# A down product of 22 feature tiles, 16 of them regrouped into seven products of quarters

## The chip, the core and the metric

The kernel runs on one NeuronCore of a Trainium2 chip. A time is device microseconds (us) of one execution. The core's engines run at the same time and wait for each other by semaphores: TensorE (PE in the profile: matmuls into PSUM, weight loads as PEld), VectorE (DVE), ScalarE (ACT), GpSimd (POOL) and SyncE (SP). Each takes its instructions strictly in the order in which they stand in its queue. SP and POOL also issue transfers (DMA) between DRAM and the on-chip buffers.

## The reference

Two layers on 512 tokens of width 1024. Each layer has a mixer (convolution and windowed attention, or gated linear attention and latent attention), a layer norm, a SwiGLU feed-forward network with 2816 hidden features, and a second layer norm:

```python
def swiglu(x, w_gate, w_up, w_down):
    return (jax.nn.silu(x @ w_gate) * (x @ w_up)) @ w_down

x = layer_norm(ALPHA * x + y, ln_mix_g[layer], ln_mix_b[layer])
x = layer_norm(ALPHA * x + swiglu(x, ffn_w_gate[layer], ffn_w_up[layer], ffn_w_down[layer]),
               ln_ffn_g[layer], ln_ffn_b[layer])
```

The change is in the last factor, `@ w_down`, of both layers: 512 tokens x 2816 features times 2816 x 1024.

## The kernel before

All arithmetic is float32. A product of two float32 tiles is made of three matmuls in a reduced 32-bit format: each operand is split into an upper part `hi` (a cast on ACT) and a lower part `lo` = operand - `hi` (a subtraction on DVE), and hi*hi, hi*lo and lo*hi are added up in PSUM. `split` (lines 96 to 104) does that: its ACT row stands at L98, its DVE row at L104. A weight tile is 128 x 1024: `weight()` fetches it from DRAM on SP into one of the 5 buffers of the pool `raw` (RAW), takes one of the 5 pairs of the pool `w` (WP) and splits it. A feature tile of the hidden activations is 128 features x 512 tokens; its parts go to the pool `hx` (HX, 12 buffers).

The feed-forward network of a layer has two stages.

- Gate and up (`ffn`, `sevens`). The first two feature tiles (DIRECT) are plain products. The other 20 are taken in ten pairs, each by Winograd's form of Strassen's method: seven products of quarters in place of eight, with sums of weight quarters and of input quarters ahead of them. `make(i)` prepares product i: a sum of weights on DVE (L531, L525), then the split. `take(i)` issues its matmuls (L553) and moves the results between PSUM banks on ACT and DVE. The loop calls `make(i)` and then `take(i - 4)` (AHEAD), so the preparation runs up to four products ahead; `make(i)` also needs the `w` pair that product i - 5 has given back. This whole stage is under `tc.manual_schedule`: the instructions of every engine stand in the order in which the code is written.
- Down (`down`). The 22 feature tiles come one by one in groups `[1] * 17 + [5]`. For each tile `prep` splits the tile and its 128 x 1024 weight tile; then for 4 blocks of 128 tokens and 2 halves of 512 columns three matmuls (L336, in `one`) add into one of 8 PSUM banks, 24 matmuls for a tile. The last group has five tiles, so that the layer norm of one block of tokens runs beside the matmuls of the next.

PE's matmuls always stand in the order of the code. The weights lie in DRAM in the order in which the kernel fetches them; `_chunks` puts them there before the launch.

## Time and profile before

| | |
|---|---|
| median of 3 runs | 1075.84 us (1075.57 to 1076.06) |
| the profiled execution | 1075.87 us; span of its instructions 1074.1 us |
| granted TensorE clock | 0.999 |
| PE busy | 1064.4 us (99%), 6957 matmuls |
| DVE, ACT, POOL busy | 726.7 us (68%), 497.9 us (46%), 61.3 us (6%) |
| transfers | 110.44 MB, 103 GB/s on average |
| matmuls of the down products and of the mixers' output products (L336) | 1425, 326.0 us busy |

How to read it: busy time is the union of an engine's instructions; matmuls overlap in the pipeline, so the mean length of one (390 ns) is longer than the step from one to the next. In the rows of a timeline stand start and length in us, engine, line, operation, output <- input, shape, count, and in brackets the time for which the engine stood idle before it and what ended that. The chain of waits follows the work that ended last back to the start, each step to what released it.

### The profile page before, as it was taken

The numbers are of one execution on the slowest core, as the hardware profiler recorded it, in microseconds if no ns is written. First come the engines' busy times: TensorE is split into PE (matmuls) and PEld (weight loads), VectorE is DVE, ScalarE is ACT, GpSimd is POOL, SyncE is SP. The second block draws the span as 40 slices with busy tenths as digits, with TensorE's granted clock in tenths as the row PEclk, the third lists the DMA queues.
The fourth block names the chain that finished last, engine by engine and source line by source line (L and its number), as shares of the span: only waits on it lengthen the run. The fifth ranks groups of instructions, "written<-read, shape, count | busy, mean of one in ns | idle before, by whom it ended". The sixth has DMA issues, their size and how long they took to land.

```text
span 1074.1 us, 17049 instructions
## 1 busy us (share of the span) xinstructions
PE 1064.4 (99%) x6957; PEld 962.6 (90%) x6957; DVE 726.7 (68%) x1128; ACT 497.9 (46%) x832; POOL 61.3 (6%) x98
## 2 busy tenths in 40 slices
PE   9999999999999999999999999999999999999997
PEld 7888889999999998888988888889999999988886
DVE  5666539897787783334857886479977777753337
ACT  5544335654544562223467453355645545542221
POOL 0000000000000000000513420000000000000001
PEclk9999999999999999999999999999999999999999
DMA  9522221333323343331332031223423323442302
GB/s 337 202 79 79 79 79 59 99 99 124 113 80 120 116 161 115 98 99 59 99 137 78 2 118 30 77 71 80 147 89 108 117 90 107 156 134 96 98 1 78
DMA packets 32078, 110.44 MB, mean 103 GB/s; under 512 B 3568, under 2 KB 4224, under 8 KB 32000
## 3 DMA queue, kind: packets, MB, share of 16 engines
q1 hardware_dynamic: 31712, 108.31, 30.5%
q0 software_dynamic: 288, 1.05, 0.6%
q8 instruction: 54, 0.88, 0.3%
q14 instruction: 24, 0.20, 0.1%
HBM read 107.25 MB, written 2.10 MB: 102 GB/s over the span
## 4 chain that ended last, share of the span: by engine, by line
PE 97%; DVE 1%; DMA 0%; ACT 0%; issue 0%; SPq 0%; POOL 0%; DVEq 0%; ACTq 0%; POOLq 0%
PE ps L553 38%; PE ps L336 29%; PE ps L180 16%; PE ps L214 6%; PE ps L1005 1%; PE ps L276 1%; PE ps L930 1%; PE ps L853 1%; PE ps L702 1%; PE ps L649 1%; PE ps L689 1%; DMA hx<-in_xT_dram 0%; PE ps L903 0%; PE ps L919 0%; PE ps L901 0%; PE ps L1080 0%
## 5 line engine op out<-in xcount | busy, mean ns | idle before, releaser
L336 PE MATMUL ps<-w,hx 128*128 128x512 f32 x1425 | 326.0, 390 | 0.0
L336 PEld LDWEIGHTS ps<-w,hx 128*128 128x128 f32 x1425 | 266.7, 188 | 55.0
L104 DVE TENSOR_TENSOR w<-raw,w 128x1024 fp32r<-128x1024 f32 (+2 forms) x182 | 219.9, 1213 | 63.9 <-ACT w L98 58.1
L553 PE MATMUL ps<-xh,w 128*128 128x256 f32 x1280 | 237.5, 283 | 0.0
L98 ACT CAST w<-raw 128x1024 fp32r<-128x1024 f32 (+3 forms) x185 | 189.6, 1032 | 60.4 <-PE ps L553 21.1
L553 PEld LDWEIGHTS ps<-xh,w 128*128 128x128 f32 x1280 | 202.7, 192 | 0.0
L553 PE MATMUL ps<-xl,w 128*128 128x256 f32 x640 | 181.2, 283 | 0.0
L553 PE MATMUL ps<-hx,w 128*128 128x256 f32 x1440 | 179.6, 283 | 0.0
L553 PEld LDWEIGHTS ps<-hx,w 128*128 128x128 f32 x1440 | 176.0, 192 | 0.1
L180 PE MATMUL ps<-xh,w 128*128 128x512 f32 (+1 forms) x608 | 161.0, 348 | 0.1
L553 PEld LDWEIGHTS ps<-xl,w 128*128 128x128 f32 x640 | 122.8, 192 | 0.3
L180 PEld LDWEIGHTS ps<-xh,w 128*128 128x128 f32 x608 | 106.4, 189 | 15.2 <-ACT xh L98 0.5
L180 PE MATMUL ps<-xl,w 128*128 128x512 f32 (+1 forms) x304 | 104.9, 345 | 0.2 <-DVE xl L104 0.2
L104 DVE TENSOR_TENSOR hx<-m,hx 128x512 fp32r<-128x512 f32 x32 | 21.4, 688 | 81.4 <-ACT hx L98 81.4
L180 PEld LDWEIGHTS ps<-xl,w 128*128 128x128 f32 x304 | 57.6, 190 | 7.0 <-DVE xl L104 0.5
L253 POOL TENSOR_TENSOR rs<-ve,neghalf 128x1 f32<-128x1 f32 x15 | 9.5, 635 | 866.7 <-DVE ve L251 828.8
L214 PE MATMUL ps<-w,xh 128*128 128x512 f32 (+1 forms) x192 | 58.6, 386 | 0.3 <-ACT lng L909 0.3
L98 ACT CAST hx<-m 128x512 fp32r<-128x512 f32 x32 | 19.2, 623 | 83.3 <-PE ps L336 83.1
L104 DVE TENSOR_TENSOR hx<-wk,hx 128x512 fp32r<-128x512 f32 x28 | 19.3, 691 | 51.8 <-ACT hx L98 51.8
L104 DVE TENSOR_TENSOR w<-lng,w 128x1024 fp32r<-128x1024 f32 x30 | 36.8, 1225 | 21.1 <-ACT w L98 21.1
L104 DVE TENSOR_TENSOR w<-lnb,w 128x1024 fp32r<-128x1024 f32 x30 | 36.8, 1225 | 17.4 <-ACT w L98 17.3
L98 ACT CAST hx<-wk 128x512 fp32r<-128x512 f32 x28 | 17.4, 622 | 64.0 <-PE ps L336 61.4
(229 smaller groups left out, 1112.2 us busy)
## 6 DMA issues: line engine op xcount, KB each, us to landing
raw<-in_w_dram SPq DMA_DIRECT2D x182, 512.0 KB, 4.1
hx<-in_xT_dram SPq DMA_DIRECT2D x8, 256.0 KB, 5.5
xn<-in_xn_dram SPq DMA_DIRECT2D x4, 512.0 KB, 9.4
out_dram<-xn SPq DMA_DIRECT2D x7, 256.0 KB, 2.0
lng<-in_ln_mix_g_dram SPq DMA_DIRECT2D x2, 512.0 KB, 7.9
lnb<-in_ln_mix_b_dram SPq DMA_DIRECT2D x2, 512.0 KB, 8.0
raw<-in_w_dram POOLq DMA_DIRECT2D x2, 512.0 KB, 5.6
lng<-in_ln_ffn_g_dram SPq DMA_DIRECT2D x2, 512.0 KB, 6.9
```

The source lines that it names most:

```text
L98: nc.scalar.copy(out=hi, in_=src)
L104: tt(out=lo, in0=src, in1=hi.bitcast(F32), op=ALU.subtract)
L180: mm(dst[:, cols], lhsT=l[:, k, :], rhs=r[:, k, cols], start=(k == 0 and n == 0), stop=(k == KD - 1 and n == 2))
L214: mm(banks[b][:, :n], lhsT=l[:, k, t], rhs=r[:, c], start=(k == 0 and m == 0), stop=(k == KD - 1 and m == 2))
L276: nc.tensor.transpose(tp[:, k * P:(k + 1) * P], xn[:, b, h * 512 + k * P:h * 512 + (k + 1) * P], ident)
L336: mm(acc[b][h], lhsT=l[:, bs], rhs=r[:, h * 512:h * 512 + 512], start=(k == 0 and n == 0), stop=(k == ends[b, h] and n == 2))
L553: mm(bank[:, f * 256:f * 256 + 256], lhsT=l[:, f, k, :], rhs=r[k // 2][:, k % 2, :], start=(start and f == 0 and k == 0 and m == 0), stop= ...
L649: mm(banks[s][bank][:, o:o + n], lhsT=l[rows[s], b * P:(b + 1) * P], rhs=r[rows[s], (b + 1) * P - n:(b + 1) * P], start=(i == 0), stop=(i ...
L689: nc.tensor.transpose(bank[:, o:o + P], src, ident)
L702: mm(po[rows[s], b * P:(b + 1) * P], lhsT=vn[:, j * P + 64 * s:j * P + 64 * s + 64], rhs=loc[s][(b, half)], start=(half == 0 or b == 0), s ...
L853: mm(dst, lhsT=x[:, c], rhs=y, start=(k == 0 and n == 0), stop=(k == nk - 1 and n == 2))
L930: mm(po[:, e * P:(e + 1) * P], lhsT=vv[j - 1 if j else i][:, h * P:(h + 1) * P], rhs=pt[e][:, j * P:(j + 1) * P], start=(j == 0), stop=(j ...
```

## The change

Of the 22 feature tiles, tiles 2 to 17 (16 tiles, 4 * QUADS) are no longer taken one by one. They make a product of 512 tokens x 2048 features x 1024 columns, which is cut into quarters: tokens in two halves of 256, features in two halves of 8 tiles, columns in two halves of 512. With A for the hidden activations and B for the weights, the seven products of Winograd's form are each summed over four groups (q = 0 to 3) of two feature tiles, 28 small products in all, in the order of the list `seq` of pairs (pos, q). `seven_down` holds it. A small product is 12 matmuls of 128 x 512 (2 blocks of tokens, 2 feature tiles, 3 parts). The sums over q stay in PSUM, and the sums between the seven products are made by continuing in a bank: after the last product of pos 6, ACT copies the two banks `d` to two banks `e` (L619) and the products of pos 3 go on in `d`; after the last of pos 7 it copies `e` to `f`, and pos 4 goes on in `f`. The sums of activation quarters are made on DVE (L581 to L588) in every `make` of pos 5, 6, 3 and 7, ahead of the split of the sum. The sums of weight quarters are running sums: after the split of one stage, a transfer on POOL's queue with `accum_op=ALU.add` adds the next quarter from DRAM to the same buffer (`add`, 16 transfers of 512 KB in a layer). The buffers of the running weight sums and of the activation sums are those of `xh` and `xl`, which is why these are now two tiles each (`xk`, `renew`). The six other feature tiles follow in `down` in groups `[1, 5]`, added to the same banks. The hidden tiles of a pair are kept as one tile for each half of the tokens, so that `half` is one instruction, not two. The first two loads of `seven_down` (`raw` of ("21", 0) and ("21", 1)) are issued when `seven_down` is called, which is before the loop over the gate and up products; the layer norm's `load_ln` moves into the loop.

```diff
+QUADS = 4
...
-    def down(hs, groups, gb, last=False, after=None, keep=None):
+    def down(hs, groups, gb, last=False, after=None, keep=None, acc=None):
...
-        nk = len(hs)
-        acc = {}
+        nk = sum(groups)
+        begun = acc is not None
+        acc = acc if begun else {}
...
-                if gi == 0:
+                if gi == 0 and not begun:
                     acc[b] = [ps(), ps()]
...
-            for i in range(AHEAD + 3, n + AHEAD):
+            acc, more, takes = seven_down(hs)
+            for i in range(AHEAD + 3, n + len(more) + AHEAD):
                 if i < n:
                     make(i)
-                take(i - AHEAD)
-        gb = load_ln("ffn", layer)
-        return down(hs, [1] * (KF - 5) + [5], gb, last)
+                elif i < n + len(more):
+                    more[i - n]()
+                    if i == n + 3:
+                        gb = load_ln("ffn", layer)
+                i -= AHEAD
+                if i < n:
+                    take(i)
+                else:
+                    takes[i - n]()
+        rest = [h for h in hs[:DIRECT]] + [h for h in hs[DIRECT + 2 * QUADS:]]
+        return down(rest, [1, 5], gb, last, acc=acc)
+
+    def seven_down(hs):
...
+        seq = [(2, 0), (2, 1), (1, 0), (1, 1), (2, 2), (5, 0), (1, 2), (5, 1), (1, 3), (2, 3), (5, 2), (6, 0),
+               (5, 3), (6, 1), (6, 2), (6, 3), (3, 0), (3, 1), (3, 2), (3, 3), (7, 0), (7, 1), (7, 2), (7, 3),
+               (4, 0), (4, 1), (4, 2), (4, 3)]
...
+        def add(t, which, q):
+            nc.gpsimd.dma_start(out=t, in_=piece(which, q), accum_op=ALU.add)
...
+        def make(i):
+
+            for args in loads.get(i, ()):
+                load(*args)
+            pos, q = seq[i]
+            (a11, a21), (a12, a22) = hs[DIRECT + q], hs[DIRECT + QUADS + q]
+            w = raw["21", q] if pos == 2 else raw["22", q] if pos in (3, 7) else t_[q]
+            hi, lo = pair()
+            split(w, hi, lo)
+            if pos in (1, 5, 6, 3):
+                add(w, {1: "12", 5: "22", 6: "21", 3: "12"}[pos], q)
+            hh, hl = slot2(F32R), slot2(F32R)
+            x = {1: a11, 2: a12, 4: a22, 7: None}.get(pos, s_.get(q))
+            if pos == 5:
+                tt(out=x, in0=a22, in1=a21, op=ALU.subtract)
+            elif pos == 6:
+                tt(out=x, in0=x, in1=a11, op=ALU.add)
+            elif pos == 3:
+                tt(out=x, in0=x, in1=a12, op=ALU.subtract)
+            elif pos == 7:
+                x = temp()
+                tt(out=x, in0=a11, in1=a21, op=ALU.subtract)
...
+                split(x, hh, hl)
+            ops[i] = hi, lo, hh, hl
+
+        def take(i):
...
+                if pos == 5:
+                    g.setdefault("p5", []).append(temp("p"))
+                    nc.scalar.copy(out=g["p5"][b], in_=bank)
+                elif pos in (6, 7):
+                    to = "e" if pos == 6 else "f"
+                    g.setdefault(to, []).append(ps())
+                    nc.scalar.copy(out=g[to][b], in_=bank)
+            if q == QUADS - 1:
+                for b in range(2):
+                    if pos == 1:
+                        g["p1"] = temp()
+                        nc.scalar.copy(out=g["p1"], in_=g["d"][b])
+                        g.setdefault("sum", []).append((b, g["p1"]))
+                    elif pos in (3, 7):
+                        bank = g[name][b]
+                        stt(out=bank, in0=bank, scalar=-1.0, in1=g["p5"][b], op0=ALU.mult, op1=ALU.subtract)
+            if pos == 2 and q == QUADS - 1:
+                for b, t in g["sum"]:
+                    tt(out=g["a"][b], in0=g["a"][b], in1=t, op=ALU.add)
...
-                for f in range(2):
-                    c = slice(f * 256, f * 256 + 256)
-                    stt(out=g["h"][f][:, n * 256:n * 256 + 256], in0=gate[:, c], scalar=-1.0, in1=up[:, c],
-                        op0=ALU.mult, op1=ALU.mult)
+                stt(out=g["h"][n], in0=gate, scalar=-1.0, in1=up, op0=ALU.mult, op1=ALU.mult)
```

Three engines, each at one place of the first layer's down stage. In these rows `w` is a weight pair, `hx` a part of an activation tile, `wk` a hidden tile, `ssum` an activation sum, `tsum` a running weight sum, `ps` a PSUM bank. The lines of the changed kernel differ from those of the profile before: its split stands at L99 and L105, its small products at L609.

ACT before, in the middle of the tiles taken one by one: the upper parts of an activation tile and of a weight tile in turn.

```order
L98 CAST hx_4478<-wk_2831 128x512
L98 CAST w_4451<-raw_4449 128x1024
L98 CAST hx_4511<-wk_2832 128x512
L98 CAST w_4484<-raw_4482 128x1024
L98 CAST hx_4544<-wk_3059 128x512
L98 CAST w_4517<-raw_4515 128x1024
```

ACT now, from the `make` of (3, 0) to that of (7, 0):

```order
L99 CAST w_4499<-raw_4401 128x1024
L99 CAST hx_4503<-ssum_4080 128x512
L615 COPY p_4514<-ps_4345 128x512
L615 COPY p_4522<-ps_4346 128x512
L99 CAST w_4524<-raw_4428 128x1024
L99 CAST hx_4528<-ssum_4080 128x512
L99 CAST w_4545<-raw_4453 128x1024
L99 CAST hx_4549<-ssum_4228 128x512
L99 CAST w_4566<-raw_4476 128x1024
L99 CAST hx_4570<-ssum_4228 128x512
L619 COPY ps_4581<-ps_4283 128x512
L619 COPY ps_4589<-ps_4284 128x512
```

The copies of `d` to `e` (L619) belong to the `take` of (6, 3), the 16th product, and stand in ACT's queue behind both casts of the `make` of (3, 3), the 20th; the cast of each activation sum stands ahead of the cast of the next weight.

DVE before, at the same tiles as ACT above:

```order
L104 TENSOR_TENSOR hx_4479<-wk_2831,hx_4478 128x512
L104 TENSOR_TENSOR w_4451<-raw_4449,w_4451 128x1024
L104 TENSOR_TENSOR hx_4512<-wk_2832,hx_4511 128x512
L104 TENSOR_TENSOR w_4484<-raw_4482,w_4484 128x1024
L104 TENSOR_TENSOR hx_4545<-wk_3059,hx_4544 128x512
```

DVE now, from the `make` of (6, 2) to that of (3, 0):

```order
L105 TENSOR_TENSOR w_4455<-tsum_4227,w_4455 128x1024
L583 TENSOR_TENSOR ssum_4228<-ssum_4228,wk_2605 128x512
L591 SCALAR_TENSOR_TENSOR hx_4460<-ssum_4228,hx_4459 128x512
L105 TENSOR_TENSOR w_4478<-tsum_4227,w_4478 128x1024
L583 TENSOR_TENSOR ssum_4228<-ssum_4228,wk_2831 128x512
L591 SCALAR_TENSOR_TENSOR hx_4483<-ssum_4228,hx_4482 128x512
L105 TENSOR_TENSOR w_4499<-raw_4401,w_4499 128x1024
L585 TENSOR_TENSOR ssum_4080<-ssum_4080,wk_3057 128x512
L105 TENSOR_TENSOR hx_4504<-ssum_4080,hx_4503 128x512
```

Each `make` now has three instructions on DVE, and the activation sum (L583, L585) stands behind the lower part of the weight and ahead of the lower part of the sum itself.

PE now, the end of (6, 3) and the start of (3, 0); before, the eight banks took 24 matmuls of one tile in turn, with no copy between:

```order
L609 MATMUL ps_4284<-w_4478,hx_4482 128x512 x2
L609 MATMUL ps_4284<-w_4478,hx_4483 128x512
L609 MATMUL ps_4284<-w_4478,hx_4482 128x512 x2
L609 MATMUL ps_4284<-w_4478,hx_4483 128x512
L609 MATMUL ps_4283<-w_4499,hx_4503 128x512 x2
L609 MATMUL ps_4283<-w_4499,hx_4504 128x512
```

(3, 0) goes on in the banks `ps_4283` and `ps_4284` that the copies of L619 read.

## The prediction

> **What bounds the kernel now.** I read the page first, then the chain of waits in order of time, then the timelines of ACT and DVE.

> ```profile
> span 1074.1 us, 17049 instructions
> PE 1064.4 (99%) x6957; PEld 962.6 (90%) x6957; DVE 726.7 (68%) x1128; ACT 497.9 (46%) x832; POOL 61.3 (6%) x98
> L336 PE MATMUL ps<-w,hx 128*128 128x512 f32 x1425 | 326.0, 390 | 0.0
> ```

> ```profile
> 219.39 181.43 PE ps L553 x1512
> 400.82 110.19 PE ps L336 x486
> 946.54 106.12 PE ps L336 x468
> ```

> PE is the bound: it is busy 99% of the span, and the matmuls of the down product wait for nothing (0.0 us idle). In the chain, 486 of them take 110.19 us, 0.2267 us each; in the second layer it is 0.2268. A gate and up product takes 24 x 181.43 / 1512 = 2.88 us. So time is saved by fewer matmuls, as long as ACT and DVE keep their operands coming. How they do that in the down stage now:

> ```profile
> 401.41 1.04 ACT L98 CAST w<-raw 128x1024 fp32r<-128x1024 f32 x1
> 406.10 0.62 ACT L98 CAST hx<-wk 128x512 fp32r<-128x512 f32 x1 [3.65 <-PE ps L336]
> 406.63 1.05 ACT L98 CAST w<-raw 128x1024 fp32r<-128x1024 f32 x1
> 411.54 0.62 ACT L98 CAST hx<-wk 128x512 fp32r<-128x512 f32 x1 [3.87 <-PE ps L336]
> ```

> ```profile
> 406.76 0.69 DVE L104 TENSOR_TENSOR hx<-wk,hx 128x512 fp32r<-128x512 f32 x1 [3.02 <-ACT hx L98]
> 407.70 1.23 DVE L104 TENSOR_TENSOR w<-raw,w 128x1024 fp32r<-128x1024 f32 x1 [0.26 <-ACT w L98]
> 412.20 0.69 DVE L104 TENSOR_TENSOR hx<-wk,hx 128x512 fp32r<-128x512 f32 x1 [3.27 <-ACT hx L98]
> ```

> One tile every 5.44 us (406.10 to 411.54), and both engines stand idle for over 3 us of it, waiting for PE. This slack is what the change spends.

> **What is saved on PE.** 16 tiles x 24 = 384 matmuls become 28 x 12 = 336: 48 fewer in a layer, 96 in all, of the same shape (128 x 512). 96 x 0.2268 = 21.8 us. A small product takes 12 x 0.2268 = 2.72 us.

> **What the preparation costs.** It must now be done every 2.72 us. The trace has the new order of work at one place, where the gate and up stage makes its input sums (DVE L414, two tiles at a time) between two weight splits:

> ```profile
> 201.34 1.28 DVE L414 TENSOR_TENSOR p<-m 128x512 f32<-128x512 f32 x2
> 204.27 1.22 DVE L104 TENSOR_TENSOR w<-raw,w 128x1024 fp32r<-128x1024 f32 x1 [0.26 <-ACT w L98]
> 205.41 1.28 DVE L414 TENSOR_TENSOR p<-tmp,m 128x512 f32<-128x512 f32 x2
> ```

> ```profile
> 202.06 1.23 ACT L98 CAST hx<-p 128x512 fp32r<-128x512 f32 x2
> 203.19 1.05 ACT L98 CAST w<-raw 128x1024 fp32r<-128x1024 f32 x1
> ```

> Sum to its cast 0.72 us; two casts 1.13 us; the weight cast to its lower part 1.08 us; that to the next sum 1.14 us; 4.07 us from sum to sum. The new `make` has one tile, whose cast takes 0.53 us (406.10 to 406.63), so its ring is 0.72 + 0.53 + 1.08 + 1.14 = 3.47 us. It is a ring since both engines take their work in order: the sum stands behind the previous weight on DVE, and the next weight's cast behind the sum's cast on ACT. 16 of the 28 makes have a sum (pos 5, 6, 3, 7), and those from the 11th to the 24th stand together, except for copies between. Each is 3.47 - 2.72 = 0.75 us slower than PE.

> That alone would eat up the lead of four products and no more. But the 17th product, (3, 0), waits for the copy of `d` to `e`, and that copy stands on ACT behind the whole make of the 20th. At this place the lead is worth nothing. Rows for the extra work:

> ```profile
> 383.58 0.57 ACT L580 COPY ps<-ps 128x512 f32<-128x512 f32 x1 [1.29 <-PE ps L553]
> 384.06 1.05 ACT L98 CAST w<-raw 128x1024 fp32r<-128x1024 f32 x1
> 397.98 1.05 ACT L98 CAST w<-raw 128x1024 fp32r<-128x1024 f32 x1 [0.22 <-PE ps L553]
> ```

> ```profile
> 398.24 0.68 DVE L601 TENSOR_TENSOR p<-p,ps 128x512 f32<-128x512 f32 x1
> 398.84 0.69 DVE L104 TENSOR_TENSOR hx<-wk,hx 128x512 fp32r<-128x512 f32 x1
> ```

> A copy holds ACT for 0.48 us, an add with PSUM holds DVE for 0.60 us. The cast at 397.98 starts 0.06 us after the product that frees its pair (the 69th of 70, which ended 2.88 us before 400.82): the preparation is at its full lead when the down stage starts. I count from the end of the gate and up products (t = 0). Up to the 11th make the lead holds: only two of those ten have a sum, and each loses 0.8 us that the next plain ones give back. So the 11th starts when the 6th product has freed its pair, at 6 x 2.72 + 0.08 = 16.4. Its sum's cast is at 16.4 + 1.08 + 1.14 + 0.72 = 19.34. Nine rings on, 9 x 3.47 = 31.23, stands the 20th's; on the way two copies `p1` (0.96) and two copies `p5` (0.96) stretch the ring on ACT, and two adds to `a` on DVE: the lower part of the sum ends 0.66 + 0.60 after its cast (406.10, 406.76), the adds 1.20 later, at 2.46, where the next weight could have gone at 0.53 + 1.08 = 1.61, so 0.85. Sum 53.34. With that cast (0.53) and the copy (0.57) PE may start (3, 0) at 54.4. It ended the 16th product at 16 x 2.72 = 43.5. **PE stands still for 10.9 us in each layer**, 21.8 us in all, which is what the matmuls save. After it PE is ahead of nothing: by then the 20th make is done, four products are ready, the rest follow at 3.47 and later (pos 4, without a sum) at some 1.75 us, before PE asks for them; the copy to `f` has 1.36 us of the other block's matmuls beside it.

> **What the standstill does to the clock.** Start and end of the program show it.

> ```profile
> 1.45 5.87 PE L147 MATMUL ps<-hx 128*128 128x512 f32 x14 [1.45 <-DVE hx L145]
> 1062.68 3.75 PE L306 MATMUL ps<-w,hx 128*128 128x256 f32 x30
> ```

> ```profile
> 1066.00:1070.00 4.00, 0.43 (x4) 1.00 0.05 20
> 1070.00:1074.00 4.00, 0.00 (x0) 0.70 0.38 133
> ```

> The last matmul ends at 1066.4, and in the last stretch the granted clock (the column behind PE's) is 0.70 on average: it fell to half some 5 us after the last matmul (0.4 of 4 us at 1, the rest at 0.5). The first 14 matmuls after a standstill take 0.42 us each, not 0.227. An idle time of 10.9 us is long enough, so the first dozen matmuls after it run at half speed: 12 x (0.427 - 0.227) = 2.4 us, taking 5.87 us as the time to recover and 0.427 for a fully slow one; twice 4.8 us. Bounds: 0 if the clock stays up, 2.8 us (14 x 0.2) each. [...]

> **Transfers.** Running sums go over POOL's queue.

> ```profile
> raw<-in_w_dram SPq DMA_DIRECT2D x182, 512.0 KB, 4.1
> raw<-in_w_dram POOLq DMA_DIRECT2D x2, 512.0 KB, 5.6
> ```

> ```profile
> 189.00:190.00 1.00, 1.00 (x11) 1.00 (x10) 1.00 (x2) 1.00 (x2) 0.00 (x0) 1.00 0.95 168
> 190.00:191.00 1.00, 1.00 (x11) 1.00 (x10) 0.74 (x2) 0.98 (x2) 0.00 (x0) 1.00 1.07 213
> ```

> An adding transfer lands after 5.6 us and keeps the DMA engines busy for some 3 us (share about 1, from 188 to 191). Needed sooner than 5.6 us? A transfer starts when the lower part of its weight is done, 1.08 + 1.14 us after that make's start. The tightest are (1, 0) to (5, 0), started at -3.5 (its make at -2 x 2.88 + 0.08) and needed at 2.8 (the sixth make, one product freed), and (1, 2) to (5, 2), 8.5 to 16.4. Alone they fit, by 0.7 and 2.3 us. But up to there seven plain loads and four adding ones want the same DMA engines. I take 0 for this term; the other end is 4 us in a layer.

> The two `raw` buffers taken early leave three for the gate and up products. A quarter is then loaded only when one of the previous group is split, two or three products (5.8 to 8.6 us) before its use, against 4.1 us to landing: 0, and if the cover goes, up to 1 us for each of 8 groups. `half` in one instruction, `load_ln` earlier, the 12 more weight splits: beside PE, or inside the ring counted above. POOL's later work (one power for each block of the layer norm) comes some 20 us after its last transfer. The last groups `[1, 5]`: their five preparations wait for the same pairs as before, 0.

> **Sum**, against the profiled 1075.87 us (0.03 over the median): 1075.9 - 21.8 + 21.8 + 4.8 = 1080.7, say 1081 us.

> **Rivals.**
> - *PE never waits* (the other side). If the ring does not close, DVE's own load decides: 1.14 + 2 x 0.60 = 2.34 us for a make with a sum, under 2.72. Then only the copy on ACT shows, about 1.4 us in a layer: 1075.9 - 21.8 + 2.8 = 1057. For it: DVE's idle 3 us of 5.44. Against it: the 0.26 us wait for ACT within the ring above. It decides if the ring is under some 3.1 us: 9 x (3.47 - 3.1) takes 3.3 us off the wait, and wait and clock then cost under 10 us in a layer.
> - *The wait comes, the clock does not fall*: 1076, no change. For it: only a start and an end show the clock, no pause. Against: 10.9 us is twice the 5 us of the end.
> - *The adding transfers come late*: 4 us more in a layer, 1089. For it: the shares of about 1; against: most of them have 8 us and more.
> - *Three buffers starve the gate and up stage*: 16 us more, 1097. Against it: SP waits 381 us in all for free buffers there now, and PE never waits for a load.

> ```profile
> SPq L506 <- DVE w L104: 381.1, 60, 21.8
> ```

> **Chances.** The forecast 54%, PE never waits (or waits less than half of it) 12%, clock stays up 14%, late transfers 15%, starved stage 5%. The range: a ring of 3.35 to 3.6 us changes the wait by 1.3 us a layer, the clock term by up to 0.8, transfers add up to 4 us a layer; with the second rival that is 1074 to 1091; the first and the last rival lie outside. Faster or slower by under 0.2% (2.2 us) is about what a measurement of this kernel cannot tell from no change: the second rival lies within it, with a part of the low end of the forecast. Faster 0.13, same 0.18, slower 0.69.

> **What would show it.** Right: in each down stage one idle time of PE of 9 to 13 us ahead of the first product of pos 3, ended by ACT's copy at L619; a dip of the granted clock behind it; sums on DVE 3.4 to 3.6 us apart before it; no other wait of PE over 1 us. Wrong: DVE's sums 2.7 us apart; PE idle while ACT waits for a transfer to `tsum`; the gate and up products longer than 2.88 us; the clock at 1.00 behind the wait.

## The result, and the profile after

The changed kernel takes 1089.1 us (median of 4 runs, 1088.67 to 1089.22) against 1075.7 us before on the same chip: ratio 1.0123, 95% interval 1.0106 to 1.0141, slower by 13.4 us. The forecast was 1081, 5.2 us slower, with a range to 1091. The profiled execution took 1089.05 us. Its page, and the group of the down product's small products:

```profile
span 1087.2 us, 17047 instructions
PE 1049.5 (97%) x6861; PEld 947.1 (87%) x6861; DVE 791.2 (73%) x1180; ACT 544.1 (50%) x896; POOL 89.2 (8%) x130
q1 hardware_dynamic: 30560, 104.12, 29.3%
q0 software_dynamic: 4896, 17.83, 9.3%
L609 PE MATMUL ps<-w,hx 128*128 128x512 f32 x672 | 159.9, 400 | 27.9 <-ACT ps L619 23.5
```

There are 96 matmuls fewer, as forecast, but PE now stands idle for 27.9 us ahead of these products, 23.5 of them until ACT's copy at L619. PE's timeline shows where (start, length, count, and in brackets the idle time before and what ended it), both layers:

```profile
400.44 30.11 PE L609 MATMUL ps<-w,hx 128*128 128x512 f32 x132
432.70 11.58 PE L609 MATMUL ps<-w,hx 128*128 128x512 f32 x48 [2.15 <-ACT tmp L624]
444.45 3.32 PE L609 MATMUL ps<-w,hx 128*128 128x512 f32 x12 [0.17 <-ACT hx L590]
459.73 34.45 PE L609 MATMUL ps<-w,hx 128*128 128x512 f32 x144 [11.97 <-ACT ps L619]
...
952.64 30.11 PE L609 MATMUL ps<-w,hx 128*128 128x512 f32 x132
984.78 15.49 PE L609 MATMUL ps<-w,hx 128*128 128x512 f32 x60 [2.03 <-ACT tmp L624]
1011.81 34.86 PE L609 MATMUL ps<-w,hx 128*128 128x512 f32 x144 [11.54 <-ACT ps L619]
```

The first product of pos 3 starts 59.3 us after the gate and up products (t = 459.73 - 400.44), not 54.4. The 144 matmuls behind the wait take 34.45 and 34.86 us instead of 144 x 0.2268 = 32.66: 1.8 and 2.2 us lost to the clock (granted 0.50 until 462.99 and until 1015.95 us, 3.3 and 4.1 us after the product starts). A second idle time of 2 us, ahead of the product that waits for the copy `p1` (L624), was not in the forecast. The chain of waits, followed back through layer 0, says what lies behind both:

```profile
401.08 10.80 DMA tsum<-in_w_dram
411.98 1.06 ACT w L99
...
418.05 10.44 DMA tsum<-in_w_dram
428.59 1.07 ACT w L99
...
454.48 0.61 DVE ssum L585
455.64 1.05 ACT w L99
456.72 1.23 DVE w L105
459.73 34.45 PE ps L609 x144
```

Its last part is the ring of the forecast. Its first part is two adding transfers that took 10.8 and 10.4 us until their weight's cast could start; the forecast had taken 0 for them. ACT's timeline shows all five casts of layer 0 that a transfer held up, the fourth of them that of the 11th make (the second waits for a plain load on SP's queue, the others for adding transfers):

```profile
404.06 1.05 ACT L99 CAST w<-tsum 128x1024 fp32r<-128x1024 f32 x1 [1.31 <-DMA tsum<-in_w_dram]
408.30 1.05 ACT L99 CAST w<-tsum 128x1024 fp32r<-128x1024 f32 x1 [0.67 <-DMA tsum<-in_w_dram]
411.98 1.05 ACT L99 CAST w<-tsum 128x1024 fp32r<-128x1024 f32 x1 [2.11 <-DMA tsum<-in_w_dram]
421.08 1.05 ACT L99 CAST w<-tsum 128x1024 fp32r<-128x1024 f32 x1 [2.60 <-DMA tsum<-in_w_dram]
428.59 1.06 ACT L99 CAST w<-tsum 128x1024 fp32r<-128x1024 f32 x1 [0.47 <-DMA tsum<-in_w_dram]
```

The 11th make starts at t = 421.08 - 400.44 = 20.6 instead of 16.4.

### The profile page after: what moved, and what is told of

It is laid out like the page before. It is cut to its first block, busy times and chain, and to the rows that moved or that the text cites. A ratio compares the mean times of both kernels' runs of the same rounds, so it can differ in the third digit from the quotient of the medians.

```text
span 1087.2 us, 17047 instructions
## 1 busy us (share of the span) xinstructions
PE 1049.5 (97%) x6861; PEld 947.1 (87%) x6861; DVE 791.2 (73%) x1180; ACT 544.1 (50%) x896; POOL 89.2 (8%) x130
## 3 DMA queue, kind: packets, MB, share of 16 engines
q0 software_dynamic: 4896, 17.83, 9.3%
## 4 chain that ended last, share of the span: by engine, by line
PE 86%; DVE 5%; DMA 5%; ACT 3%; issue 1%; SPq 0%; POOL 0%; DVEq 0%; ACTq 0%; POOLq 0%
PE ps L712 35%; PE ps L189 15%; PE ps L345 13%; PE ps L609 7%; PE ps L223 6%; DMA tsum<-in_w_dram 4%; DVE w L105 2%; ACT w L99 2%; PE ps L1161 1%; PE ps L285 1%; PE ps L1086 1%; PE ps L1009 1%; PE ps L858 1%; PE ps L805 1%; PE ps L845 1%
## 5 line engine op out<-in xcount | busy, mean ns | idle before, releaser
L105 DVE TENSOR_TENSOR w<-raw,w 128x1024 fp32r<-128x1024 f32 (+2 forms) x174 | 210.0, 1211 | 60.3 <-ACT w L99 55.7
L99 ACT CAST w<-raw 128x1024 fp32r<-128x1024 f32 (+3 forms) x177 | 181.4, 1032 | 65.7 <-PE ps L712 18.1
L609 PE MATMUL ps<-w,hx 128*128 128x512 f32 x672 | 159.9, 400 | 27.9 <-ACT ps L619 23.5
L609 PEld LDWEIGHTS ps<-w,hx 128*128 128x128 f32 x672 | 129.1, 193 | 58.1 <-ACT ps L619 24.4
L345 PE MATMUL ps<-w,hx 128*128 128x512 f32 x657 | 151.9, 391 | 0.0
L345 PEld LDWEIGHTS ps<-w,hx 128*128 128x128 f32 x657 | 122.7, 188 | 25.1
L559 POOL DMA_DIRECT2D tsum<-in_w_dram x24 | 20.9, 871 | 493.4 <-DVE w L105 282.1
L105 DVE TENSOR_TENSOR w<-tsum,w 128x1024 fp32r<-128x1024 f32 x32 | 39.2, 1224 | 18.1 <-ACT w L99 18.1
L105 DVE TENSOR_TENSOR w<-lng,w 128x1024 fp32r<-128x1024 f32 x30 | 36.7, 1223 | 17.1 <-ACT w L99 16.9
L105 DVE TENSOR_TENSOR w<-lnb,w 128x1024 fp32r<-128x1024 f32 x30 | 36.7, 1223 | 15.0 <-ACT w L99 14.9
L105 DVE TENSOR_TENSOR hx<-m,hx 128x512 fp32r<-128x512 f32 x32 | 21.4, 689 | 31.8 <-ACT hx L99 31.8
## 6 DMA issues: line engine op xcount, KB each, us to landing
raw<-in_w_dram SPq DMA_DIRECT2D x166, 512.0 KB, 4.3
tsum<-in_w_dram POOLq DMA_DIRECT2D x24, 512.0 KB, 8.4
raw<-in_w_dram POOLq DMA_DIRECT2D x10, 512.0 KB, 5.7
tsum<-in_w_dram SPq DMA_DIRECT2D x8, 512.0 KB, 6.3
xn<-in_xn_dram SPq DMA_DIRECT2D x4, 512.0 KB, 9.4
lng<-in_ln_mix_g_dram SPq DMA_DIRECT2D x2, 512.0 KB, 7.7
```

What stands on the lines that cost most here:

```text
L99: nc.scalar.copy(out=hi, in_=src)
L105: tt(out=lo, in0=src, in1=hi.bitcast(F32), op=ALU.subtract)
L345: mm(acc[b][h], lhsT=l(b), rhs=r[:, h * 512:h * 512 + 512], start=(not begun and k == 0 and n == 0), stop=(k == ends[b, h] and n == 2), sk ...
L559: nc.gpsimd.dma_start(out=t, in_=piece(which, q), accum_op=ALU.add)
L609: mm(bank, lhsT=l[:, t], rhs=r[:, c], start=(fresh and k == 0 and m == 0), stop=(k == 1 and m == 2), skip_group_check=True)
```

## The experiments

Ten kernels, in three sets; each set ran on one chip beside the kernel before, and each ratio is to that. (Between the sets the median of the kernel before varies from 1075.5 to 1076.1 us, so a difference between two sets can be off by some 0.5 us.) e1 to e6 start from the changed kernel, e7 to e10 from e4.

| run | what it changes | us (median) | ratio to before (95%) |
|---|---|---|---|
| e1 | no adding transfers | 1081.5 | 1.0047 (1.0032 to 1.0061) |
| e2 | the loads of the quarters 22 later | 1083.6 | 1.0066 (1.0049 to 1.0082) |
| e3 | the copies d to e ahead of the 19th make | 1089.3 | 1.0122 (1.0106 to 1.0137) |
| e4 | the ring opened | 1060.2 | 0.9846 (0.9831 to 0.9861) |
| e5 | plain transfers in place of adding ones | 1081.4 | 1.0051 (1.0036 to 1.0066) |
| e6 | matmuls in PE's standstill | 1085.4 | 1.0091 (1.0075 to 1.0106) |
| e7 | e4, and (2, 3) later | 1065.4 | 0.9898 (0.9882 to 0.9915) |
| e8 | e7 and e2 | 1056.4 | 0.9823 (0.9808 to 0.9838) |
| e9 | e4 and e2 | 1063.2 | 0.9884 (0.9866 to 0.9902) |
| e10 | e9, and the copies d to e ahead of the 20th make | 1054.8 | 0.9813 (0.98 to 0.9827) |

**e1, without the adding transfers.**

```diff
-            if pos in (1, 5, 6, 3):
+            if False:
                 add(w, {1: "12", 5: "22", 6: "21", 3: "12"}[pos], q)
```

> The adding transfers are left out, so the running weight sums are not formed and the output differs; every other instruction stands where it stood in the changed kernel. Theory (the adding transfers make the 11th make of a down stage late): no cast of a summed weight waits for a transfer, the 11th make starts at t = 16.4 instead of 20.6 us after the gate and up products, the first product of pos 3 at t = 54 instead of 59.3; 2 x 4.9 us less, with the smaller clock loss 1077 to 1081 us. What is left against the kernel before (PE standing still for 11 us and the clock behind it) stays. Rival (the lateness comes from the load on ACT and DVE, not from transfers): 1086 to 1090 us.

1081.5 us, 7.6 less than the changed kernel (8.0, if each is compared with the kernel before in its own set). PE's waits and its timeline in layer 0:

```profile
PE ps L609 <- ACT ps L619: 21.9, 2, 11.0
```

```profile
400.78 43.71 PE L609 MATMUL ps<-w,hx 128*128 128x512 f32 x192
455.46 34.95 PE L609 MATMUL ps<-w,hx 128*128 128x512 f32 x144 [10.97 <-ACT ps L619]
```

The first 16 products run without a pause, pos 3 starts at t = 54.7, and PE stands still for 21.9 us in all: the 54.4 and the 21.8 of the forecast. The clock behind the two waits (granted 0.986 over this run, 0.998 to 0.999 before) costs 2.3 us here (34.95 - 32.66) and 3.0 in layer 1 (35.70 us for 144 matmuls). So the ring and the copy behind it were sized right, and what the sum lacked came with the transfers.

**e2 and e5, why the transfers are late.** e2 leaves all transfers in and moves four plain loads; e5 leaves all of them where they are and takes only the adding away.

```diff
-            nc.sync.dma_start(out=raw[which, q], in_=piece(which, q))
+            (nc.gpsimd if which == "22" else nc.sync).dma_start(out=raw[which, q], in_=piece(which, q))
```

> Only the four plain loads of the quarters 22 move, from SP's queue, where all four start within 4 us after the gate and up products, to POOL's, where each stands behind the adding transfer of the make before it (the 12th to 15th). All transfers are made. Theory (adding transfers land late because these plain loads share the DMA engines with them): the adding transfers of the first 20 us land in 6 to 8 us instead of 8.4 and more, the 11th make starts 2 to 4 us earlier, 1081 to 1085 us. Rival (an adding transfer is itself that slow, or is delayed by the three plain loads that stay and by POOL): the wait of the 11th make stays over 2 us, 1087 to 1090 us.

```diff
-            nc.gpsimd.dma_start(out=t, in_=piece(which, q), accum_op=ALU.add)
+            nc.gpsimd.dma_start(out=t, in_=piece(which, q))
```

> The 24 adding transfers become plain ones of the same 512 KB, on the same queue, at the same places, with the same waits; the weight sums are not formed, so the output differs. Theory (it is the time that adding takes on the DMA engines, 328 ns for a 4 KB piece against 159 ns for a plain one in the trace of the changed kernel, that fills them in the first 20 us): they land in 5 to 7 us instead of 8.4, casts no longer wait for them by more than 1 us, 1080 to 1084 us. Rival (the number of transfers and their bytes fill the queue, adding or not): the 11th make stays 3 us or more late, 1087 to 1090 us.

1083.6 and 1081.4 us: both recover most of it, e5 as much as leaving the transfers out, with landings even earlier than the 5 to 7 us expected. The transfers' rows (KB each, median us from issue to landing) of the changed kernel, e2 and e5, in this order:

```profile
tsum<-in_w_dram POOLq DMA_DIRECT2D x24, 512.0 KB, 8.4
```

```profile
tsum<-in_w_dram POOLq DMA_DIRECT2D x24, 512.0 KB, 6.8
```

```profile
q0 software_dynamic: 4896, 17.83, 5.1%
tsum<-in_w_dram POOLq DMA_DIRECT2D x24, 512.0 KB, 4.1
```

The rows count the 24 transfers of a run that add to `tsum`; eight more add to `raw` (pos 3), and e1 and e5 concern all 32, not 24 as was expected of e5. So neither theory's rival holds, and the two theories are one: it is a matter of the engines' time. The page gives the mean length of a packet: 9.3% x 16 engines x 1087.2 us / 4896 packets = 330 ns for a queue of nearly only adding transfers; in e5, with the same packets and bytes, 5.1% x 16 x 1078.2 / 4896 = 180 ns. One packet in nine has only 4 bytes; of the 4 KB pieces alone the median in the changed kernel's trace is 328 ns adding (POOL's queue) and 159 ns plain (SP's). A transfer of 512 KB is 128 pieces, so some 2.6 us of all 16 engines against 1.4. (POOL's own time to issue one, 0.87 us against 0.54 in e5, is too small a difference to make up the 4.3 us between the landings.) The windows of layer 0 from 400 to 430 us (last columns: granted clock, busy share of the DMA engines, GB/s), of the changed kernel:

```profile
400.00:410.00 10.00, 10.00 (x49) 8.34 (x48) 6.99 (x9) 5.29 (x7) 1.75 (x2) 1.00 0.98 232
410.00:420.00 10.00, 10.00 (x46) 8.29 (x45) 7.20 (x9) 4.61 (x6) 2.62 (x3) 1.00 1.05 288
420.00:430.00 10.00, 10.00 (x46) 8.29 (x45) 5.45 (x8) 4.32 (x5) 1.74 (x2) 1.00 1.06 266
```

The DMA engines are full (shares of 0.98 to 1.06). An estimate from these lengths: from 398.3, when the first of them is issued, to 421.1, when the 11th make starts, six adding transfers (6 x 2.64 = 15.8 us) and seven plain loads (7 x 128 x 0.167 / 16 = 9.4 us, from q1's row) ask for 25.2 us in 22.8. By the trace's packets, pieces of 4.6 adding and 6.0 plain transfers were begun in that stretch and took 21.9 us of the 16 engines; the rest had to wait. Taking four plain loads out (5.3 us) brings the demand under the time there is, and so does plain in place of adding (6 x 1.2 = 7.2 us), with more to spare: in e2 one cast of layer 0 and three of layer 1 still wait 0.3 to 1.5 us for a transfer to `tsum`, in e5 none.

**e3, the copies earlier.**

```diff
+                if i == n + 18:
+                    for j in range(n + 14, n + 16):
+                        takes[j - n]()
...
-                else:
+                elif not n + 14 <= i < n + 16:
                     takes[i - n]()
```

> Only the place of the copies d to e (with the products (6, 2) and (6, 3) on PE, whose order stays) moves, from behind the 20th make to ahead of the 19th. Theory (the first product of pos 3 waits for a copy that stands on ACT behind makes that have nothing to do with it, and these run at 3.47 us each): the copy starts 6.9 us earlier (452.2 instead of 459.1), the product with it; later makes then come 0.6 to 0.8 us late each for the next products, so 10 to 14 us less in all, 1075 to 1080 us. Rival (ACT and DVE are simply too slow for 28 makes, wherever the copy stands): PE waits as long as before, only at other products; 1086 to 1090 us.

1089.3 us: no gain, though pos 3 does start 7 us earlier (the copy is L622 here). PE's group and its layer 0:

```profile
L612 PE MATMUL ps<-w,hx 128*128 128x512 f32 x672 | 165.4, 408 | 22.2 <-ACT ps L622 17.7 <-ACT tmp L627 4.3 <-ACT hx L593 0.2
```

```profile
452.43 24.59 PE L612 MATMUL ps<-w,hx 128*128 128x512 f32 x96 [5.05 <-ACT ps L622]
481.03 12.77 PE L612 MATMUL ps<-w,hx 128*128 128x512 f32 x48 [4.01 <-ACT ps L622]
```

The time came back twice. PE now reaches the end of pos 7 before the copy of `e` to `f`, which stands on ACT behind the last makes, those of pos 7 and pos 4: 4.0 us of idle time that the late start had hidden. And there are two waits of 4 to 5 us instead of one of 12, each followed by matmuls at half clock (granted 0.50 from 450.70 to 457.53 and from 481.42 to 484.83 us): 24.59 - 96 x 0.2268 = 2.8 us and 12.77 - 48 x 0.2268 = 1.9 us, against 1.8 once. In all, 5.7 us less idle (22.2 for 27.9) and 5.5 us more busy (165.4 for 159.9). My expectation had followed the ring to the 24th make and forgotten the second copy behind it. By time alone this run fits the rival, "too slow wherever the copy stands"; e4 refutes that.

**e4, the ring opened.** The same instructions; only the sum of the next make stands ahead of this make's lower part on DVE.

```diff
-            split(w, hi, lo)
+            nc.scalar.copy(out=hi, in_=w)
+            if i + 1 < len(seq) and seq[i + 1][0] in (5, 6, 3, 7):
+                xs[i + 1] = sum_of(*seq[i + 1])
+            tt(out=lo, in0=w, in1=hi.bitcast(F32), op=ALU.subtract)
```

> The activation sum of the next make is put on DVE ahead of the lower part of this make's weight, so the cast of a sum on ACT no longer waits for it; same instructions, same number. Theory (the ring sum, cast, next weight's cast, its lower part limits, at 3.47 us, and not what the engines have to do): sums come 2.3 to 2.8 us apart, PE waits at most 1 to 5 us in a layer (the copy d to e and what the late transfers leave), the clock stays up, 1055 to 1064 us, faster than both kernels. Rival (DVE with three or four passes in a make, or ACT, is itself the bound): sums still 3.2 us or more apart, 1080 us or more.

1060.2 us, faster than both kernels. DVE's sums, first of the changed kernel, then of e4:

```profile
450.94 0.69 DVE L585 TENSOR_TENSOR ssum<-ssum,wk 128x512 f32<-128x512 f32 x1
454.40 0.69 DVE L585 TENSOR_TENSOR ssum<-ssum,m 128x512 f32<-128x512 f32 x1
```

```profile
440.54 0.68 DVE L575 TENSOR_TENSOR ssum<-ssum,wk 128x512 f32<-128x512 f32 x1
442.88 0.69 DVE L575 TENSOR_TENSOR ssum<-ssum,m 128x512 f32<-128x512 f32 x1
```

3.46 us apart with the ring, 2.34 without: the forecast's figure for DVE's own load (1.14 + 2 x 0.60). The transfers are no earlier here (8.9 us to landing, casts wait up to 5.7 us for them), but a preparation that takes 2.34 us for a product of 2.72 regains its lead, and only the copy d to e (L628) is left to wait for, as PE's waits show (us in total, times, longest):

```profile
PE ps L618 <- ACT ps L628: 4.2, 2, 2.1
```

**e6, what the clock cost.** 40 matmuls whose results nobody reads fill most of the standstill.

```diff
+                    elif pos == 6 and b == 1:
+                        for j in range(40):
+                            mm(g["b"][j % 2], lhsT=hh[:, :P], rhs=hi[:, :512], start=True, stop=True)
```

> 40 matmuls of the same shape, whose results nothing reads, stand on PE between the 16th product and the first of pos 3 (some 9.1 us of the 12 in which it stands still). Theory (the clock falls because PE rests): no dip of the granted clock behind the wait, the 144 matmuls after it take 32.7 us instead of 34.5 and 34.9, the start of the first product of pos 3 stays where it was: 3 to 5 us less, 1084 to 1086 us. Rival (the clock is not what makes these matmuls long): 1088 to 1090 us.

1085.4 us, 3.7 less. The product of pos 3 starts when it did (t = 59.2), and its 144 matmuls take 32.94 us; in the window in which the 40 run, the granted clock (the column ahead of the DMA share) stays at 1.00:

```profile
448.11 9.63 PE L628 MATMUL ps<-w,hx 128*128 128x512 f32 x40 [0.17 <-ACT p L615]
459.47 32.94 PE L609 MATMUL ps<-w,hx 128*128 128x512 f32 x144 [1.74 <-ACT ps L619]
```

```profile
448.00:458.00 10.00, 9.63 (x40) 7.43 (x40) 6.88 (x9) 4.63 (x7) 1.77 (x3) 1.00 0.83 140
```

**e7 to e10, what is left of the waits.** e7 moves one product, e8 and e9 use e2's late loads, e10 the copies' place for one make:

```diff
-seq = [..., (1, 3), (2, 3), (5, 2), (6, 0), (5, 3), (6, 1), (6, 2), (6, 3), (3, 0), ...
+seq = [..., (1, 3), (5, 2), (6, 0), (5, 3), (6, 1), (6, 2), (6, 3), (2, 3), (3, 0), ...
```

```diff
+                if i == n + 19:
+                    for j in range(n + 15, n + 16):
+                        takes[j - n]()
...
-                else:
+                elif not n + 15 <= i < n + 16:
                     takes[i - n]()
```

> The open ring, and the product (2, 3) moved from the 10th place to the 16th, between (6, 3) and (3, 0), which does not depend on it; its accumulation into a is not needed before. Theory (the 4.2 us of waits and the clock dip that the open ring leaves come from the copy d to e alone): 2.72 us of matmuls now stand beside the copy, PE waits for nothing over 0.5 us, 1052 to 1056 us. Rival (ACT or DVE is late there anyway): PE waits 2 us as before, 1058 to 1061 us.

> As the run before, and the four loads of the quarters 22 stand behind adding transfers on POOL's queue. Theory (with the ring open, the lead of four products hides late transfers): no difference to the run before beyond 1 us, 1052 to 1056 us. Rival (late transfers still reach PE): 1 to 4 us less than the run before.

> The open ring and the late loads of the quarters 22, with (2, 3) in its old place. Theory (what e7 lost was the copy p1, which the move of (2, 3) brought one product nearer to the product that waits for it, behind makes held up by late transfers): no wait for p1; the copy d to e still costs 1 to 2 us in a layer, with or without a dip of the clock behind it: 1056 to 1060 us. Rival (moving (2, 3) is a gain by itself once the loads come late): 2 us or more above the 1056.4 us measured with it.

> As the run before, and the copies d to e stand on ACT ahead of the 20th make instead of behind it. Theory (what the open ring leaves is the copy's place behind a make): the copy starts as soon as the 16th product is done, PE waits 0.2 to 0.8 us in a layer ahead of the first product of pos 3 and nowhere else, no dip of the clock, 1054 to 1057 us. Rival (as in e3, the time comes back at a later product): PE waits over 1 us for a make behind the copy, 1057 to 1060 us.

e7 did not do what its theory said: 1065.4 us, 5 more than e4. The wait for the copy d to e is gone, as meant, but one of another kind has come:

```profile
PE ps L618 <- ACT tmp L633: 7.5, 2, 4.5
```

```profile
427.80 1.05 ACT L590 CAST w<-tsum 128x1024 fp32r<-128x1024 f32 x1 [4.57 <-DMA tsum<-in_w_dram]
430.75 1.05 ACT L633 COPY tmp<-ps 128x512 f32<-128x512 f32 x2
```

Product (6, 0) needs the copy `p1`, and only one product is now left between (1, 3), whose result is copied, and (6, 0). The copy stands on ACT behind a make that waits 4.57 us for its adding transfer. With late loads the same order has no such wait, and 1056.4 us (e8). That run's theory had expected no difference: here late transfers did reach PE, and cost 9 us, more than its rival had given.

e9 did not do it either: 1063.2 us, where 1056 to 1060 was expected; PE waits 2.1 and 4.0 us for the copy d to e, in layer 1 behind a make whose own cast waits 2.2 us for a load, and the clock falls in both layers (34.56 and 34.40 us for 144 matmuls; granted 0.995 over the run), so the move of (2, 3) is a gain once the loads come late. The late loads alone are a loss with the ring open: e9 is 3 us slower than e4 (ratios 0.9884 and 0.9846, whose intervals do not meet). The loads on POOL's queue now land after 10.1 us instead of 6.3 (median of `raw` there), and a make that has no lead to spare waits for them.

e10 puts that copy ahead of the make and does what its theory expected: 1054.8 us, 1.87% under the kernel before. With e8, from which its interval does not separate it, it is the fastest:

```profile
PE ps L621 <- ACT ps L631: 0.2, 1, 0.2
```

```profile
L621 PE MATMUL ps<-w,hx 128*128 128x512 f32 x672 | 153.0, 389 | 0.2 <-ACT ps L631 0.2
```

672 matmuls in 153.0 us, 0.2277 each, with 0.2 us of idle time.

## What the prediction had right, and the step that failed

- *PE saves 21.8 us*: right. e10 runs the same 28 products without waits at 1054.8 us, 20.7 under the kernel before (1075.54 in that set); the profiled span fell by 21.0.
- *The ring of 3.47 us, and 10.9 us of standstill by the copy behind the 20th make*: right in place, cause and size. The ring measured 3.46, and e1 gives 21.9 us of standstill for 21.8. That DVE's load is not the limit, which the prediction had left to a rival, e4 shows.
- *Adding transfers cost 0*: **this step failed**. Without them the kernel takes 7.6 us less (8.0 within the sets), 3.8 to 4 a layer: the other end that was named (4 us) and the rival's 1089. The sign of being wrong that the prediction gave for it, ACT waiting for a transfer to `tsum`, is in the trace (up to 2.60 us). The prediction checked each transfer by itself ("alone they fit, by 0.7 and 2.3 us"), saw that eleven transfers want the same engines, and did not add up their time. The page before had both lengths: 0.6% x 16 x 1074.1 / 288 packets = 360 ns on POOL's queue, 30.5% x 16 x 1074.1 / 31712 = 165 ns on SP's. With them the four adding transfers ask for 4 x 128 x 0.360 / 16 = 11.5 us and the seven plain loads for 9.2, together 20.8 us in the 19.9 from -3.5 to 16.4: the engines have no time left over in which a transfer could be late without harm. The seven plain loads were all issued within 4 us at the very start, four of them for quarters that no make before the 17th reads:

```profile
400.63 0.81 SPq L553 DMA_DIRECT2D tsum<-in_w_dram  x2
401.49 2.94 SPq L556 DMA_DIRECT2D raw<-in_w_dram  x5
```

- *The clock, 2.4 us a layer*: right in kind; 1.8 and 2.2 us behind the long waits, and the removal of these two gains 3.7 (e6) for 4.8. The clock came back 3.3 and 4.1 us after PE did, not 5.87. In layer 1 a further 1.9 us came behind the 2-us wait for `p1` (60 matmuls in 15.49 us). No run shows the 0.8 us by which the range lets the clock term vary: the 1.8 and 2.2 us measured lie 0.6 and 0.2 us under the 2.4.
- *Starved gate and up stage*: did not happen; 1440 of its matmuls take 172.81 us, 0.120 each, as 1512 did in 181.43.
- In sum: idle 27.9 for 21.8, and 6.6 us of longer matmuls for 4.8: 1.8, 1.9 and 2.2 by the clock and 0.7 in layer 0 (48 matmuls in 11.58 us). In these PE had caught up with the ring, and its weight loads for (6, 2) wait for the two parts of that product's activation sum, 0.26 and 0.43 us:

```profile
440.99 0.30 PEld L609 LDWEIGHTS ps<-w,hx 128*128 128x128 f32 x2 [0.26 <-ACT hx L590]
441.71 2.15 PEld L609 LDWEIGHTS ps<-w,hx 128*128 128x128 f32 x10 [0.43 <-DVE hx L591]
```

That is 7.9 of the 8.2 us by which the forecast fell short. Without the adding transfers the forecast's 1081 stands (e1: 1081.5).
- *A slip of the prediction that changes nothing*: the cast at 397.98 starts 0.04 us after the product that frees its pair (400.82 - 2.88), not 0.06.

## What to carry to other kernels

When a change gives transfers to a queue, add up the DMA engines' time over the stretch before each deadline, from the packets' length by kind (here 330 ns adding, 180 ns plain on the same queue) and from when the issuing queue really gets to issue them, not transfer by transfer. Look for rings across two in-order engines: here the same instructions in another order on DVE turned 13 us lost into 16 us gained. And before moving a wait, follow it to the end of the stage: the next copy behind the same queue, and the clock behind the pause, took it all back in e3: 5.7 us less idle, 5.5 us more busy.

## What was unexpected of the hardware

A piece of 4 KB that adds to its destination takes a DMA engine 328 ns in the changed kernel's trace, a plain one on SP's queue there 159 ns (medians); in e5, with plain transfers on POOL's queue, the mean packet of that queue takes 180 ns instead of 330. And the granted clock fell to 0.50 behind a pause of PE of only 2.03 us. Two windows of the changed kernel, after the same wait in layer 0 (2.15 us) and in layer 1 (2.03 us):

```profile
434.00:435.00 1.00, 1.00 (x6) 0.84 (x5) 0.88 (x1) 0.08 (x1) 0.00 (x0) 1.00 1.02 201
```

```profile
986.00:987.00 1.00, 1.00 (x4) 0.81 (x3) 0.80 (x1) 0.17 (x1) 0.00 (x0) 0.50 1.06 209
```

One fell, one did not. In e4 it fell behind the first of the two pauses: 34.54 us for 144 matmuls behind 2.15 us of idle time in layer 0 (granted 0.50 from 449 to 451), 32.98 behind 2.09 in layer 1.
